# Weight sums moved into the attention in 2 KB pieces, and a scheduler's table of durations changed, in a two-layer diffusion block on one core

## The chip, the core and the metric

One NeuronCore of one Trainium2 chip runs the whole program in one launch. The metric is the time of one execution in microseconds (us) on the device. Five queues of instructions run beside each other: PE (matrix products), DVE and POOL (elementwise work), ACT (activations, scaled copies) and SP, which here only issues DMAs. POOL issues DMAs too. All DMAs of both queues share 16 DMA engines.

## The reference, cut to what matters

Two layers over 1024 latent and 256 context tokens of width 1024. Each projects the modulated input, runs latent attention (4 heads) and differential attention (4 heads) and a chunk mixer side by side, projects back, normalizes, and ends with a gated feed-forward block of inner width 2816 with a depthwise convolution of width 3:

```python
def conv_ffn(h, p):
    u = dwconv3(h @ p["ffn_wup"], p["ffn_convw"], p["ffn_convb"])
    gate, val = jnp.split(u, 2, axis=-1)
    return (jax.nn.silu(gate) * val) @ p["ffn_wdown"]

def layer(x, xc, mod, modc, rows, cols, p, layer_idx, need_ctx):
    sh1, sc1, g1, sh2, sc2, g2 = jnp.split(mod, 6, axis=-1)
    ...
    y, yc = mixer(x * (1.0 + sc1) + sh1, xc * (1.0 + csc1) + csh1, rows, cols, p, layer_idx, need_ctx)
    x = layer_norm(DN_ALPHA * x + g1 * y, p["ln1_g"], p["ln1_b"])
    x = layer_norm(DN_ALPHA * x + g2 * conv_ffn(x * (1.0 + sc2) + sh2, p), p["ln2_g"], p["ln2_b"])
```

`mod` comes from one more product, of the conditioning vector with `ada_w`; most of its columns are computed in pieces between the blocks of the attention.

## The kernel before, in words

Every fp32 product is three products of a high and a low half (`mm3`): each operand is copied into a high half (a rounding copy, on ACT or DVE; helpers `copy` L460 and `move` L466) and a low half (full minus high, helper `low` L457, on DVE or POOL). PE's own calls are all in the helper `mm` (L447).

The two feed-forward products use seven block products in place of eight (a scheme of Strassen's kind). That needs sums and differences of blocks of the weights. They are not computed on an engine: POOL issues DMAs that copy a block from DRAM to DRAM (L592, a copy) and then add another block into it (L593, an accumulating DMA; it waits for its copy, or for another sum). The arrays are `ws` for the first product and `db` for the second; each layer has 32 DMAs for `ws` and 16 for `db`, each of 1408 KB (`SUMROWS` rows of the flattened array). Later SP loads `ws` and `db` like any weight.

When the sums are issued: `sums` makes a list of calls (`self.due`) and `begin_sums(1)` takes the next. Before the change the `ws` of layer 0 begin in the input projection (every fourth tile, outside `z`) and go on as fillers in its attention; the `db` of layer 0 and the `ws` of layer 1 are issued in the first feed-forward product of layer 0 (`ffn`), the rest of the latter in the input projection and the attention of layer 1; the `db` of layer 1 in the first feed-forward product of layer 1. The key `MODKEY` puts them behind about 120 later pieces of work.

What sets the order: nothing is written out by hand. `Sched.run` is a list scheduler that runs while the program is built. Each piece of work is a task with a list of engines that may take it and a duration on each, from small formulas (`act_t`, `dve_t`, `pool_t`, `either` for DVE or POOL, `psum_copy` for ACT or DVE). It keeps a clock for each engine, and a free engine takes the ready task with the lowest key. The order so found is fixed in the program: on the chip each engine runs its list in order and waits on semaphores. So a formula changes no work, only which engine does a task, and when it stands in the list. A POOL DMA is a task of 1.0 us that is done 40 us later.

Other lines that the text names: L1018 and L1024 rotate the keys into a buffer whose store to `zd` must land before the buffer is used again; L1237 and L1238 join the two score maps of the differential attention on POOL, and L1262 is PE's transposition of the result; L1640 and L1650 combine products of the first feed-forward product out of PSUM; L1671 and L1673 are its convolution (ACT, then DVE); L1490 is elementwise work of the feed-forward block (DVE or POOL), among it the combinations that `store_pair` writes to `da`.

## Time and profile before

| | |
|---|---|
| time, median of 3 runs (us) | 3523.48 (3515.53 to 3527.67) |
| the profiled execution: its time, its span (us) | 3522.21, 3520.4 |
| granted TensorE clock, mean | 0.957 |
| PE busy (us, share) | 3210.6 (91%) |
| DVE | 2586.0 (73%) |
| ACT | 1652.2 (47%) |
| POOL | 1045.3 (30%) |
| DMA: SP's queue, POOL's queue (share of 16 engines) | 34.1%, 15.9% |

The page cuts the span into 40 slices. The stages, read from the first and the last instruction of lines that belong to one stage alone: input projection of layer 0 up to 312 us, attention to 870, output projection to 1020, first feed-forward product to 1670, second to about 1925, then layer 1: input projection to 2183, attention to 2670, output projection to 2795, first feed-forward product to 3265, second to the end. PE is the busiest engine in every stage; what it does not do in a stage stands in its idle time and in the share of the clock that it was granted.

### The profile page before, as it was taken

The page shows a single profiled execution, that of the slowest core. Times are in us where ns is not written, and L with a number is a line of the kernel's source. Part 1 is how long each engine was busy: PE and PEld are TensorE (multiplying, and loading weights), DVE is VectorE, ACT ScalarE, POOL GpSimd, SP SyncE. Part 2 cuts the span into 40 slices and gives each one's busy share as a digit, 9 for nine tenths or more (in the row PEclk, how much of TensorE's full clock was granted, in tenths as well). Part 3 has the DMA queues.
Part 4 walks back from the last instruction along what each step waited for, and adds up shares of the span by engine and source line. Part 5 has one row for each costly group of instructions (what it writes and reads, how often), then busy time and mean ns, then how long its engine had stood idle before and what let it go on. Part 6 is the DMA issues. An engine that isn't in the chain of part 4 may idle for free. (4 is left out here: it accounts for less than half of the span.)

```text
span 3520.4 us, 53639 instructions
## 1 busy us (share of the span) xinstructions
PE 3210.6 (91%) x18953; PEld 2801.2 (80%) x18953; DVE 2586.0 (73%) x6262; ACT 1652.2 (47%) x2931; POOL 1045.3 (30%) x678
## 2 busy tenths in 40 slices
PE   7799999998988889989998899999998889999997
PEld 5798888787977777777886799888888867788775
DVE  7456988988777566657569737889898776666687
ACT  5024666565344344434435404566663445454543
POOL 3101555553122111213034301454434232212143
PEclk9899999999999999999999999999998999999998
DMA  8823444443345666664765743132313556653672
GB/s 324 206 65 100 116 120 131 120 106 104 111 145 168 191 176 181 191 173 147 225 217 188 213 130 78 49 77 82 89 53 121 163 157 200 201 163 132 222 263 102
DMA packets 274839, 528.07 MB, mean 150 GB/s; under 512 B 67465, under 2 KB 119177, under 8 KB 264585
## 3 DMA queue, kind: packets, MB, share of 16 engines
q1 hardware_dynamic: 263048, 386.22, 34.1%
q0 software_dynamic: 11520, 138.42, 15.9%
q8 instruction: 149, 2.44, 0.3%
q14 instruction: 122, 0.99, 0.1%
HBM read 444.25 MB, written 218.69 MB: 188 GB/s over the span
## 5 line engine op out<-in xcount | busy, mean ns | idle before, releaser
L447 PE MATMUL t<-region 128*128 128x256 f32 (+4 forms) x15631 | 2876.0, 342 | 233.4 <-DVE region L457 69.7
L447 PEld LDWEIGHTS t<-region 128*128 128x128 f32 x15631 | 2458.0, 194 | 584.9 <-DVE region L457 82.6
L457 DVE TENSOR_TENSOR region<-region 128x512 fp32r<-128x512 f32 (+6 forms) x867 | 765.2, 907 | 267.8 <-ACT region L460 225.0
L460 ACT ACTIVATE region<-t 128x512 fp32r<-128x512 f32 (+4 forms) x935 | 452.6, 511 | 717.1 <-PE t L447 326.0
L460 ACT ACTIVATE region<-region 128x512 fp32r<-128x512 f32 (+4 forms) x944 | 591.2, 662 | 384.8 <-PE t L447 131.9
L457 POOL TENSOR_TENSOR region<-region 128x512 fp32r<-128x512 f32 (+5 forms) x289 | 403.9, 1408 | 1123.2 <-ACT region L460 804.6
L1490 POOL TENSOR_TENSOR region<-region 128x512 f32<-128x512 f32 (+2 forms) x107 | 212.0, 1984 | 911.3 <-ACT region L460 355.2
L1673 DVE SCALAR_TENSOR_TENSOR region<-region,conv 128x1023 f32<-128x1023 f32 x176 | 233.4, 1327 | 165.6 <-ACT region L1671 165.3
L1198 ACT ACTIVATE region<-region,q 128x1280 f32<-128x1280 f32 (+1 forms) x216 | 273.5, 1267 | 165.2 <-DVE q L1197 148.7
L1193 DVE TENSOR_SCALAR_CACHE_REDUCE region<-t 128x512 f32<-128x512 f32 (+1 forms) x600 | 333.6, 586 | 9.4 <-PE t L447 8.0
L457 DVE TENSOR_TENSOR region<-t,region 128x512 fp32r<-128x512 f32 (+1 forms) x529 | 297.8, 598 | 46.4 <-ACT region L460 41.6
L1262 PE MATMUL t<-ident,region 128*128 128x128 f32 x1312 | 186.1, 285 | 19.9 <-DVE region L1193 5.0
L1238 POOL TENSOR_TENSOR region<-region 128x1280 f32<-128x1280 f32 (+1 forms) x69 | 188.4, 2731 | 5.8
L1262 PEld LDWEIGHTS t<-ident,region 128*128 128x128 f32 x1312 | 154.9, 147 | 27.6 <-DVE region L1193 8.2
L1671 ACT ACTIVATE region<-region,conv 128x1024 f32<-128x1024 f32 x88 | 109.2, 1241 | 128.2 <-DVE region L1654 56.7
L1237 POOL TENSOR_SCALAR region<-region,q 128x1280 f32<-128x1280 f32 (+1 forms) x69 | 87.4, 1267 | 205.6 <-DVE q L1232 128.2
L447 PE MATMUL t<-region,s 128*4 128x256 f32 x768 | 118.2, 291 | 17.2 <-ACT region L460 10.8
L1490 DVE TENSOR_TENSOR region<-region 128x512 f32<-128x512 f32 (+2 forms) x150 | 113.3, 760 | 18.4 <-POOL region L1490 15.3
L1018 DVE TENSOR_TENSOR region<-t,region 128x256 f32<-128x256 f32 x32 | 13.6, 424 | 126.5 <-PE t L447 69.6
L447 PEld LDWEIGHTS t<-region,s 128*4 128x4 f32 x768 | 64.8, 87 | 46.4 <-ACT region L460 11.3
L548 POOL TENSOR_TENSOR region<-region 128x1024 f32<-128x1024 f32 x26 | 72.8, 2815 | 93.3 <-DMA region<-n 65.6
L1688 ACT ACTIVATE region<-region 128x1024 f32<-128x1024 f32 x66 | 53.4, 839 | 63.9 <-DVE region L1673 63.9
(137 smaller groups left out, 1849.5 us busy)
## 6 DMA issues: line engine op xcount, KB each, us to landing
ws<-in_wup POOLq DMA_DIRECT2D x48, 1408.0 KB, 9.8
region<-ws SPq DMA_DIRECT2D x176, 256.0 KB, 3.7
region<-in_ada_w SPq DMA_DIRECT2D x160, 256.0 KB, 3.5
region<-in_wup SPq DMA_DIRECT2D x154, 256.0 KB, 3.0
da<-region SPq DMA_DIRECT2D x154, 256.0 KB, 3.7
region<-da SPq DMA_DIRECT2D x154, 256.0 KB, 4.0
db<-in_w_down POOLq DMA_DIRECT2D x24, 1408.0 KB, 8.5
ws<-ws POOLq DMA_DIRECT2D x16, 1408.0 KB, 14.3
```

Of the source, the lines that this page charges most:

```text
L447: self.nc.tensor.matmul(ps, a, b, start=start, stop=stop, skip_group_check=again)
L457: eng.tensor_tensor(out=out, in0=full, in1=hi.bitcast(F32), op=ALU.subtract)
L460: self.nc.scalar.activation(out, in_, AF.Copy, **kw)
L548: self.task(engs or pool_t(D), lambda e, row=row, op=op: self.vec[e].tensor_tensor(out=x[:, :D], in0=x[:, :D], in1=row.t, op=op), [x, row] ...
L1193: self.task(dve_t(b - a), lambda e: nc.vector.tensor_scalar(p[:, a:b], ps[:, :b - a], -scale, None, op0=ALU.mult, op1=ALU.min, accum_out=n ...
L1198: self.task(act_t(nk, 0.19), lambda e: nc.scalar.activation(p[:, :nk], p[:, :nk], AF.Exp, bias=m.t, scale=-1.0, accum_out=s.t), [p, m], [p ...
L1237: nc.gpsimd.tensor_scalar(p2[:, :nk], p2[:, :nk], cc.t, 0.0, op0=ALU.mult, op1=ALU.add)
L1238: nc.gpsimd.tensor_tensor(out=p1[:, :nk], in0=p1[:, :nk], in1=p2[:, :nk], op=ALU.add)
L1262: nc.tensor.transpose(ps[:, u, j * P:(j + 1) * P], B[key][j][:, (kt + u) * P:(kt + u + 1) * P], self.ident)
L1490: self.task(either(n), lambda e: self.vec[e].tensor_tensor(out=o(), in0=a(), in1=b(), op=op), r, w, **kw)
L1671: self.task(act_t(n, 0.15), lambda e: nc.scalar.activation(t.t, u(0, n), AF.Identity, scale=c[:, 1:2], bias=c[:, 3:4]), r + ["conv"], [t])
L1673: self.task(dve_t(n - 1, extra=0.06), lambda e, d=d: nc.vector.scalar_tensor_tensor(t[:, 1 - d:n - d], u(d, n - 1 + d), c[:, 2 * d:2 * d + ...
```

## The change

Three things. (1) The sums of a layer, `ws` and `db`, are all issued among the fillers of that layer's attention; the calls in the input projection and in the feed-forward block are gone. (2) Their arrays are seen as rows of 512 numbers (2 KB), 704 to a DMA, for copies and accumulations alike. The bytes and the number of DMAs stay. Before, a copy stood as 32 rows of 11264 numbers and an accumulation as 176 rows of 2048. The memory that holds the descriptors of POOL's DMAs grows from 1024 to 2048 bytes. (3) The formulas of durations: POOL from 2.1 to 2.5 ns per element, DVE in `either` and for the weights of the first product from 1.042 to 1.35, ACT's high halves from 0.833 to 1.03, the convolution longer.

```diff
-SUMROWS = 176
+SUMROWS = 704
...
 def pool_t(n):
-    return {"pool": 2.1e-3 * n + 0.15}
+    return {"pool": 2.5e-3 * n + 0.15}
...
+def act_r(n):
+    return {"act": 1.03e-3 * n + 0.09}
+def dve2_t(n):
+    return dve_t(n, 1.35e-3)
 def either(n):
-    return {**dve_t(n), **pool_t(n)}
+    return {**dve2_t(n), **pool_t(n)}
...
     def flat(self, x, c):
-        return x.rearrange("n p c -> (n p c)").rearrange("(r c) -> r c", c=2048)[c * SUMROWS:(c + 1) * SUMROWS]
+        return x.rearrange("n p c -> (n p) c")[c * SUMROWS:(c + 1) * SUMROWS]
...
-            out.append(lambda: self.s.add({"pool": 1.0}, lambda e: self.nc.gpsimd.dma_start(out=put(), in_=self.flat(a(), c)), (), **kw))
-            out.append(lambda: self.s.add({"pool": 1.0}, lambda e: self.nc.gpsimd.dma_start(out=put(), in_=self.flat(b(), c), accum_op=ALU.add, max_dma_last_dim=8192), [*r, key], **kw))
+            out.append(lambda: self.s.add({"pool": 1.0}, lambda e: self.nc.gpsimd.dma_start(out=put(), in_=self.flat(a(), c), max_dma_last_dim=2048), (), **kw))
+            out.append(lambda: self.s.add({"pool": 1.0}, lambda e: self.nc.gpsimd.dma_start(out=put(), in_=self.flat(b(), c), accum_op=ALU.add, max_dma_last_dim=2048), [*r, key], **kw))
...
-            if name != "z" and n % 4 == 1:
-                self.begin_sums(1)
...
-            if f >= 2 and (x[1] == "22" or l == 0 and f % 2 and x[1] == "S2"):
-                self.begin_sums(1)
...
+            self.due = self.sums(l, "ws") + self.sums(l, "db")
...
-    nc = _bacc.Bacc("TRN2", target_bir_lowering=False, num_devices=1, dynamic_dma_scratch_size=1024)
+    nc = _bacc.Bacc("TRN2", target_bir_lowering=False, num_devices=1, dynamic_dma_scratch_size=2048)
```

How it moves instructions, at three places on POOL. In the rows below `region` is any working buffer and `q` a column of statistics (a number behind a name tells buffers apart), `ws` and `db` are the arrays of sums; lines of the changed program are 6 to 8 higher (L457 is L465, L592 and L593 are L600 and L601, L1237 and L1238 are L1243 and L1244, L1490 is L1496).

POOL at the start of the program (input stage), before:

```order
L457 TENSOR_TENSOR region<-region 128x1024 x3
L592 DMA ws<-in_wup 32x11264 x5
L457 TENSOR_TENSOR region<-region 128x768
L457 TENSOR_TENSOR region<-region 128x256 x4
L457 TENSOR_TENSOR region<-region 128x1280
L457 TENSOR_TENSOR region<-region 128x768
L457 TENSOR_TENSOR region<-region 128x1280
L457 TENSOR_TENSOR region<-region 128x768
L592 DMA ws<-in_wup 32x11264
```

POOL at the same place, of the change:

```order
L465 TENSOR_TENSOR region<-region 128x1024 x6
L465 TENSOR_TENSOR region<-region 128x256
L465 TENSOR_TENSOR region<-region 128x768
L465 TENSOR_TENSOR region<-region 128x256 x4
L465 TENSOR_TENSOR region<-region 128x1280
L465 TENSOR_TENSOR region<-region 128x768
L465 TENSOR_TENSOR region<-region 128x1280
L465 TENSOR_TENSOR region<-region 128x768
L465 TENSOR_TENSOR region<-region 128x1280
```

The five copies at the start, and the sixth a little later, have left; the low halves follow each other. The first sum of the change stands behind the input projection.

POOL in the middle of the attention of layer 0, before:

```order
L1237 TENSOR_SCALAR region_8793<-region_8793,q_8899 128x1280
L1238 TENSOR_TENSOR region_8765<-region_8765,region_8793 128x1280
L1237 TENSOR_SCALAR region_8843<-region_8843,q_8944 128x1280
L1238 TENSOR_TENSOR region_8817<-region_8817,region_8843 128x1280
L457 TENSOR_TENSOR region_2796<-region_6044,region_8554 128x512
L593 DMA ws_91<-ws_91 176x2048
L457 TENSOR_TENSOR region_8554<-region_7603,region_2796 128x512
L457 TENSOR_TENSOR region_5388<-region_6044,region_353 128x512
L1237 TENSOR_SCALAR region_8992<-region_8992,q_9152 128x1280
L1238 TENSOR_TENSOR region_6044<-region_6044,region_8992 128x1280
L1237 TENSOR_SCALAR region_9055<-region_9055,q_9230 128x1280
L1238 TENSOR_TENSOR region_7812<-region_7812,region_9055 128x1280
```

POOL in the attention of layer 0, of the change, where the sums of `ws` run out and the first of `db` begins:

```order
L1243 TENSOR_SCALAR region_6307<-region_6307,q_6400 128x1280
L1244 TENSOR_TENSOR region_6274<-region_6274,region_6307 128x1280
L601 DMA ws_91<-ws_91 704x512
L465 TENSOR_TENSOR region_5291<-region_4597,region_5550 128x512
L601 DMA ws_91<-in_wup 704x512 x2
L600 DMA ws_91<-in_wup 704x512
L465 TENSOR_TENSOR region_2787<-region_6109,region_5496 128x512
L465 TENSOR_TENSOR region_2837<-region_6129,region_2786 128x512
L465 TENSOR_TENSOR region_3008<-region_6129,region_5856 128x512
L600 DMA db_93<-in_w_down 704x512
L465 TENSOR_TENSOR region_3199<-region_6109,region_3198 128x512
L465 TENSOR_TENSOR region_6665<-region_4597,region_6665 128x2x2x32 x2
```

Both pieces begin at the joins of a block of the attention. Before, one DMA stands between the joins of this block and those of the next; of the change five stand behind the joins, three of them with no work between. Counted over the whole order, 48 stand in either attention, where the attentions had 14 and 5 by the trace.

POOL in the first feed-forward product of layer 0, before:

```order
L1490 TENSOR_TENSOR region_10068<-region_10068,region_11779 128x1024
L1490 TENSOR_TENSOR region_11580<-region_10068 128x512
L1490 TENSOR_TENSOR region_12303<-region_12303,region_11620 128x1024
L1490 TENSOR_TENSOR region_11779<-region_12303,region_11779 128x128
L1490 TENSOR_TENSOR region_12035<-region_11779,region_12035 128x128
L1490 TENSOR_TENSOR region_11580<-region_12035,region_10068 128x512
L592 DMA db_93<-in_w_down 32x11264
L1490 TENSOR_TENSOR region_11580<-region_11580,region_11620 128x1024
L593 DMA db_93<-db_93 176x2048
L592 DMA db_93<-in_w_down 32x11264
L1490 TENSOR_TENSOR region_12783<-region_12783,region_11620 128x1024
```

POOL at the same place, of the change:

```order
L1496 TENSOR_TENSOR region_11248<-region_11248 128x1024
L1496 TENSOR_TENSOR region_11640<-region_12059,region_11640 128x128
L1496 TENSOR_TENSOR region_10412<-region_11673,region_11248 128x512
L1496 TENSOR_TENSOR region_11248<-region_10412,region_11673 128x512
L1496 TENSOR_TENSOR region_11640<-region_11248 128x512
L1496 TENSOR_TENSOR region_10412<-region_10412,region_11248 128x1024
L1496 TENSOR_TENSOR region_12826<-region_10412 128x512
L1496 TENSOR_TENSOR region_12889<-region_12889 128x1024
```

The DMAs have left, and more of the combinations of 512 columns stand on POOL. Over the whole program 28 of these go from DVE to POOL, and 27 high halves out of PSUM of 512 columns (L466) go from DVE to ACT.

## Rows read from the trace of the kernel before

**Rows 1.** The whole core by stages, one row each: attention of layer 0, the first feed-forward product of layer 0, attention of layer 1, the first feed-forward product of layer 1. A row gives the stretch in us, its length, then for each engine the busy time and the number of instructions, and last the granted TensorE clock, the busy share of the 16 DMA engines and GB/s.

```profile
312.00:870.00 558.00, 514.01 (x3594) 457.54 (x3594) 493.97 (x1466) 346.14 (x685) 269.74 (x185) 0.96 0.41 113
1020.00:1670.00 650.00, 579.38 (x2894) 484.72 (x2893) 422.26 (x520) 273.19 (x445) 144.16 (x102) 0.96 0.61 175
2183.00:2670.00 487.00, 448.60 (x3124) 400.93 (x3125) 434.68 (x1242) 300.57 (x560) 219.95 (x131) 0.96 0.29 81
2795.00:3265.00 470.00, 439.77 (x1907) 355.87 (x1907) 319.22 (x362) 232.97 (x356) 110.51 (x60) 0.97 0.57 175
```

**Rows 2.** The DMA view of the stretch from 45 to 180 us: the two queues (q0 is the one that POOL issues on, q1 that of SP) with packets, MB and share of the 16 engines' time, and one group of issues with its median us from issue to landing.

```profile
q0 software_dynamic: 1728, 21.63, 59.6%
q1 hardware_dynamic: 6095, 10.19, 22.9%
zd<-region SPq DMA_DIRECT2D x7, 128.0 KB, 33.6
```

**Rows 3.** The DMA view of the attention of layer 0 (312 to 870 us): SP's queue.

```profile
q1 hardware_dynamic: 42761, 42.07, 25.6%
```

**Rows 4.** The timeline of POOL from 108 to 176 us, some of its rows in order: start, us, engine, line, operation, count, and in brackets the idle time ahead of it and what ended that.

```profile
110.56 1.90 POOL L593 DMA_DIRECT2D ws<-in_wup  x2
125.39 0.88 POOL L593 DMA_DIRECT2D ws<-in_wup  x1 [6.67 <-issue]
125.98 3.25 POOL L457 TENSOR_TENSOR region<-region 128x1280 fp32r<-128x1280 f32 x1
141.18 0.88 POOL L593 DMA_DIRECT2D ws<-ws  x1 [6.66 <-issue]
```

**Rows 5.** The timeline of DVE from 118 to 175 us, one row.

```profile
171.41 0.43 DVE L1018 TENSOR_TENSOR region<-t,region 128x256 f32<-128x256 f32 x1 [39.83 <-DMA zd<-region]
```

**Rows 6.** The timeline of PE, nine rows that follow an idle stretch (in brackets: its length and what ended it).

```profile
83.99 1.94 PE L447 MATMUL t<-region 128*128 128x64 f32 x8 [6.72 <-issue]
90.34 1.94 PE L447 MATMUL t<-region 128*128 128x64 f32 x8 [4.41 <-issue]
172.50 3.74 PE L447 MATMUL t<-region 128*128 128x256 f32 x16 [19.43 <-DVE region L1024]
977.42 7.75 PE L447 MATMUL t<-region 128*128 128x256 f32 x45 [7.80 <-ACT region L460]
1030.95 4.23 PE L447 MATMUL t<-region 128*128 128x512 f32 x17 [3.21 <-DVE region L457]
1544.85 3.36 PE L447 MATMUL t<-region 128*128 128x512 f32 x7 [7.72 <-DVE region L1650]
2011.92 4.37 PE L447 MATMUL t<-region 128*128 128x64 f32 x14 [10.66 <-DVE q L499]
2809.72 2.50 PE L447 MATMUL t<-region 128*128 128x256 f32 x10 [4.34 <-ACT region L460]
2897.95 2.50 PE L447 MATMUL t<-region 128*128 128x512 f32 x5 [4.79 <-DVE region L1650]
```

**Rows 7.** Four more stretches in the view by windows: 18 us in the input stage, 8 us in the first feed-forward product of layer 0, the end of that stage, and the greater part of the same stage in layer 1.

```profile
80.00:98.00 18.00, 9.59 (x34) 8.48 (x35) 18.00 (x64) 2.08 (x3) 8.95 (x5) 0.53 0.43 147
1186.00:1194.00 8.00, 5.14 (x15) 4.13 (x16) 5.12 (x7) 2.89 (x5) 0.00 (x0) 0.57 0.69 237
1584.00:1670.00 86.00, 81.08 (x405) 67.38 (x405) 63.94 (x73) 42.87 (x70) 26.95 (x16) 1.00 0.47 145
2904.00:3260.00 356.00, 348.91 (x1506) 280.67 (x1505) 236.47 (x274) 178.14 (x266) 73.83 (x36) 1.00 0.57 175
```

**Rows 8.** The DMA view of the first feed-forward product of layer 0 (1020 to 1670 us) and of layer 1 (2795 to 3265 us): the stores of the gated product, median us to landing last.

```profile
da<-region SPq DMA_DIRECT2D x74, 256.0 KB, 9.9
da<-region SPq DMA_DIRECT2D x72, 256.0 KB, 2.3
```

**Rows 9.** The view of waits in the first feed-forward product of layer 0: who waited for whom, us in total, times, longest.

```profile
PE t L447 <- DVE region L1650: 36.3, 8, 7.7
ACT region L1671 <- DMA da<-region: 48.7, 8, 11.6
```

**Rows 10.** The timeline of POOL from 1168 to 1190 us: two issues.

```profile
1171.74 0.55 POOL L592 DMA_DIRECT2D db<-in_w_down  x1
1172.28 0.95 POOL L593 DMA_DIRECT2D db<-in_w_down  x1
```

**Rows 11.** The source view of the two issuing lines in the attention of layer 0: duration of the issuing instruction in ns (min/median/max), first and last start, and for each line the us to landing (min/median/max).

```profile
L592 POOL DMA_DIRECT2D ws<-in_wup x7: 553/581/587, 352.2 to 689.7; - x7
DMA to landing us min/median/max: 6.0/7.4/7.7
L593 POOL DMA_DIRECT2D ws<-ws x4: 891/907/946, 462.9 to 764.7; - x4
DMA to landing us min/median/max: 9.9/10.1/10.7
```

**Rows 12.** The view of waits in the attention of layer 0 and in that of layer 1: PE waiting for POOL's half of the joins, the whole list of PE's waits for POOL over 0.5 us.

```profile
PE t L1262 <- POOL region L1238: 0.8, 1, 0.8
PE t L1262 <- POOL region L1238: 3.5, 1, 3.5
```

**Rows 13.** Groups by line and form over the whole span, and the source view of line 466 in the attention of layer 0: the two operations that change their engine.

```profile
L1490 POOL TENSOR_TENSOR region<-region 128x512 f32<-128x512 f32 x60 | 93.2, 1556 | 184.2 <-ACT region L1515 75.3 <-DVE region L457 26.5 <-DVE q L478 18.1
L466 DVE CAST region<-t x56: 666/679/692, 364.6 to 842.2; 128x512 fp32r<-128x512 f32 x56
```

More of the change, by code (lines that the diff above doesn't have):

```diff
@@ L362 @@
 HI_EMIT = dve_fast
-HI_W = act_t
+HI_W = act_r
 HI_PV = psum_copy
@@ L468, in split @@
     def split(self, n, hi, lo, full, r, wh, wl, engs=None, high=None, **kw):
-        self.task(high or act_t(n), lambda e: self.move(e, hi(), full()), r, [wh], **kw)
+        self.task(high or act_r(n), lambda e: self.move(e, hi(), full()), r, [wh], **kw)
         self.task(engs or dve_t(n), lambda e: self.low(self.vec[e], lo(), full(), hi()), list(r) + [wh], [wl], **kw)
@@ L591, in make @@
             kw = dict(w=[key], key=MODKEY, late=40.0)
-            out.append(lambda: self.s.add({"pool": 1.0}, lambda e: self.nc.gpsimd.dma_start(out=put(), in_=self.flat(a(), c)), (), **kw))
-            out.append(lambda: self.s.add({"pool": 1.0}, lambda e: self.nc.gpsimd.dma_start(out=put(), in_=self.flat(b(), c), accum_op=ALU.add, max_dma_last_dim=8192), [*r, key], **kw))
-        for c in range((NF if which == "ws" else NP) * P * 512 // (SUMROWS * 2048)):
+            out.append(lambda: self.s.add({"pool": 1.0}, lambda e: self.nc.gpsimd.dma_start(out=put(), in_=self.flat(a(), c), max_dma_last_dim=2048), (), **kw))
+            out.append(lambda: self.s.add({"pool": 1.0}, lambda e: self.nc.gpsimd.dma_start(out=put(), in_=self.flat(b(), c), accum_op=ALU.add, max_dma_last_dim=2048), [*r, key], **kw))
+        for c in range((NF if which == "ws" else NP) * P * 512 // (SUMROWS * 512)):
             at = lambda n: (which, l, n, c)
@@ L616, in sum_chunks @@
         a, b = f * P * 512, (f + 1) * P * 512 - 1
-        m = SUMROWS * 2048
+        m = SUMROWS * 512
         return [(name, l, n, c) for c in range(a // m, b // m + 1)]
@@ L899, in in_chunk @@
             tiles = (8, 9, 0, 1) if l == 0 else (6, 7, 8, 9, 2, 3, 4, 5)
-        for n, t in enumerate(tiles):
-            if name != "z" and n % 4 == 1:
-                self.begin_sums(1)
+        for t in tiles:
             r = self.in_tile(l, name, t, wk, wb, tabs)
@@ L1587, in up_operand @@
         raw, self.up_raw[m] = self.up_raw[m], None
[L1588 removed]
+        self.blocks[f][n] = self.parts(HALF, lambda: raw.t, [raw], engs=dve2_t(HALF))
     def up_mm(self, ps, x, y, first, acq=(), h=None):
@@ L1797, in ffn @@
         last = order[-1][1]
-        assert not self.due
-        self.due = self.sums(l, "db") + (self.sums(1, "ws") if l == 0 else [])
         done = 0
@@ L1907, in program @@
         self.first_hT()
-        self.due = self.sums(0, "ws")
         for l in range(DEPTH):
```

5 lines of the change are left out of this document (2 added, 3 removed).

## The prediction, made before the run

> **What bounds the kernel now.** I read the windows by stage first. In both attentions and in both first feed-forward products PE is busy for over nine tenths of the stretch, or just under it [rows 1], so the kernel can only gain what PE loses: its idle time, and the time in which its clock is granted at 0.5. In the first product of layer 0 that is 650 - 579.4 = 70.6 us of idle time. Then the DMA view, because POOL's queue is what the change rearranges. From 45 to 180 us POOL's queue holds 59.6% of the 16 engines' time and SP's 22.9%, and a store to `zd` needs 33.6 us to land [rows 2]. What that does stands in two timelines: DVE stands still for 39.83 us because a `zd` store has not landed and its buffer is not free [rows 5], and PE behind it for 19.43 us at 172.5 us [rows 6]. Last, the timeline of PE gap by gap. The large gaps stand behind sums: POOL issues two at 1171.74 and 1172.28 us [rows 10], and 10 to 17 us later the clock is at 0.57 and PE works 5.14 of 8 us [rows 7]. In the same stage the stores to `da` land after 9.9 us, against 2.3 us in layer 1 [rows 8]; ACT waits 48.7 us for them, and PE 36.3 us, in eight gaps, for the DVE line L1650 that stands behind ACT's convolution [rows 9].
>
> Why a sum starves SP's loads and stores: its pieces are long. Before, a copy has 32 pieces of 45 KB, an accumulation 176 of 8 KB, while a 256 KB load has pieces of 2 KB. [...]
>
> **The change part by part.**
>
> *Sums leave the start, the projections and the feed-forward products.* What can come back is the gaps behind sums, and half of PE's busy time at a clock near 0.5 right after them. Input stage and projection of layer 0: 6.72 + 4.41 + 19.43 = 30.6 us of gaps; in the 18 us at 0.53, 9.59 us busy, of which 4.5 would go at full clock [rows 6, 7], and some 2 us more behind the third gap, as an estimate from the same row. At most 37; I take 30, since SP's own loads fill the engines at first. Output projection of layer 0: 7.80 us and about 2 at half clock; I take 8. First product of layer 0: eight gaps from the one that ends at 1030.95 (3.21) to the one at 1544.85 (7.72) [rows 6]. As a check from the other side, the end of that stage, after the last sum, has PE busy 81.08 of 86 us at a clock of 1.00 [rows 7]. At that rate the stage would idle 5.7% of 650 = 37 us in place of 70.6, and the clock would rise from 0.96 to 1.00, worth up to 4% of 579 = 23: 57 in all. I take 48. Input projection of layer 1: 10.66 and about 2; I take 11. First product of layer 1: gaps from 4.34 to 4.79 [rows 6], four of them, of some 15 us together by those two bounds, and about 6 at half clock; I take 18. From 2904 us on that stage works at 348.91 of 356 us with sums still in it [rows 7], so nothing more is there, and it shows that a sum does not always cost PE. Sum taken: 115 us. Bounds: about 60 (half of the gaps were due to something else) and 140.
>
> *48 sums in either attention, where 14 and 5 stood.* The issuing instruction costs POOL 0.58 us for a copy and 0.91 for an accumulation [rows 11]; for four to 22 times as many pieces it is between that and, by the step of 0.33 us over 144 more pieces (here 528 to 672 more), about 2.1. That alone is 48 x 0.75 = 36 to 100 us per attention on an engine that is busy for 270 of 558 and 220 of 487 us [rows 1]; the cover is there.
>
> The price that I look at most is room. After two accumulations at 110.56 us, POOL does not issue the third until 125.39 us, sits idle for 6.67 us of that with "issue" as the only reason, and holds a ready subtraction (L457 at 125.98) behind it; the same again at 141.18 [rows 4]. Two accumulations of 11 pieces per engine fit, the third waits until the first has landed. The change has 44 pieces per engine in twice the room: one accumulation fits, two do not, and a copy beside it is near the edge. So sums go nearly one at a time, and POOL, which issues in order, stands still when the next comes early. A copy lands after 7.4 us, an accumulation after 10.1 [rows 11]. Going through POOL's order of the change with these, and with the mean durations of its work between two sums (on average 5.4 us in layer 0, that is 270 less its 14 issues, over 48; 4.5 in layer 1), 25 and 27 of the 48 have to wait, 8 us each: about 200 us in layer 0 and 215 in layer 1. POOL is then taken for 260 + 36 + 200 = 496 of 558 us and 216 + 36 + 215 = 467 of 487. It does not become longer than the attention, but it is nearly full.
>
> Who waits behind it: low halves of weights and queries, and the joins, for PE. At present PE waits for the joins 0.8 and 3.5 us in the two attentions [rows 12], so they are ready in good time and a delay of some us is mostly hidden. For what PE loses I take 1 us for each of the 52 waits, 55 with the clock after it, from between nothing (all hidden) and 150 (SP's 25.6% [rows 3] stretches each landing by a quarter and an issue costs 2.1 us: POOL needs about 600 and 580 us, 45 and 90 beyond the present stages, and some for clock). It is nearer to nothing, because a wait of 8 us falls on an engine that has been idle half the time.
>
> *Pieces of 2 KB.* The bytes stay, so I price a copy and an accumulation as they are. Were the price one per piece and not per byte, an accumulation would take four times 10.1 us; against that, SP moves its 256 KB in 2 KB pieces and lands in 2.3 us at 8 pieces per engine [rows 8], under 0.3 us for each, at most 44 x 0.3 = 13 us for 44. That upper end lies in the 150.
>
> *Durations.* 27 high halves of 0.679 us go from DVE to ACT, 18 us, and 28 combinations to POOL at 1.556 us, 44 us [rows 13], in stages where POOL is busy for 144 of 650 and 111 of 470 us [rows 1]. DVE, at 494 of 558 us in the attention of layer 0, gets air. What a new order makes of that I can't price; I take nothing, from -15 to +20.
>
> [...]
>
> Sum: 3522.2 (the time of the profiled execution; its span is 3520.4, and the median of the runs is 1.3 above it) - 115 + 55 = 3462 us.
>
> **The rivals.** (a) *POOL's waits are hidden*: the attention loses 0 to 20 us, the rest comes back: about 3400 to 3425 us. For it: the joins wait for nobody. Against it: five sums in a row behind one block. (b) *POOL becomes the bound in the attention*: landings of 12 to 13 us instead of 10, so that POOL's list is longer than the attention's other work; the place is the pair of accumulations without work between. It decides from a loss of 126 us on, that is when each of the 52 waits costs PE 2.2 us; at 150 to 200 us it gives 3557 to 3607. [...] (c) *Half and half*: the gaps in the feed-forward products have other reasons (in layer 1 the same sums cost nothing from 2904 us on), 60 us come back and 60 go: about 3522. (d) *The sums don't matter outside*: only the input stage gains, 30 us, against 55: about 3547.
>
> **How the numbers follow.** Two executions differ by some 0.3%, or 10.6 us; less than that is no change here. Chances: the forecast (3430 to 3500 us) 0.46, (a) 0.20, (c) 0.12, (b) 0.17, (d) 0.05. Faster is the forecast and (a), 0.66; same is (c), 0.12; slower is (b) and (d), 0.22. The likeliest case's own range is 3430 to 3500. For 8 in 10 the range takes in most of (a) and the near half of (b): 3390 to 3565.
>
> **What the profile of the changed kernel would show.** Right: no DVE wait on a `zd` store in the input stage; stores to `da` landing after about 2 to 3 us in both layers; PE's waits for L1650's line gone, and the clock at 1.00 through most of the first products; these two stages 45 and 20 us shorter; POOL idle before its sums with "issue" for about 200 us in either attention, and both attentions 20 to 35 us longer. Wrong: stage times outside the attention as before, gaps of PE in the first product without a sum near them; or attentions over 60 us longer, with PE waiting for POOL's joins or low halves in tens of us; or landings of 2 KB accumulations above 13 us.

## The result, and the profile after

The changed kernel takes 3570.9 us (median; 3567.5 to 3576.2) against 3524.4 us before: a ratio of 1.0137 (95% interval 1.0114 to 1.0161). It is slower by 1.4%, 6 us above the upper end of the range.

| | after |
|---|---|
| the profiled execution: its time, its span (us) | 3567.46, 3565.7 |
| granted TensorE clock, mean | 0.945 |
| PE, DVE, ACT, POOL busy | 90%, 72%, 47%, 31% |
| DMA: SP's queue, POOL's queue | 33.6%, 16.9% |

All the work is still there, and PE's busy time is 12 us longer than before; the loss is waiting, and the lower clock around it. The table gives the length of each stage in us, in the traces of the kernels of this study (e1 to e14 are the experiments below). The boundaries are read from the first or last instruction of one line per stage (numbers of the kernel before): the last of the norm of the latent keys (L955) ends the projection, the last of L1193 the attention, the first of L1640 the output projection, its last the first product, the last of L1768 the second; in layer 1 that stage goes on to the end of the span. By these boundaries the two first products before are 44 and 49 us shorter than in [rows 1], and the attentions 10 us shorter and 1 us longer.

```
                       layer 0                      layer 1
                       in   att   out  up  down     in   att  out  up  down   span
before                 308  548   185  606  266     265  488  167  421  268   3520
after                  280  655   183  525  270     260  536  185  400  271   3566
e1  old durations      285  652   182  531  268     257  555  180  411  273   3594
e2  new durations      296  542   190  542  276     266  486  160  413  270   3442
e3  room 4096          284  597   183  525  270     260  533  184  401  272   3511
e4  8 KB pieces        283  625   183  525  271     260  578  182  404  271   3581
e5  16 rows            284  550   185  525  269     260  468  181  401  274   3397
e6  before + 2 KB      293  554   185  541  267     271  492  160  412  267   3441
e7  all but the move,  286  542   191  538  272     257  487  157  402  272   3404
    room 4096
e9  half rows          284  559   183  525  271     260  479  179  404  270   3415
e10 all but the move   294  540   187  523  275     278  488  157  402  273   3416
e8  new durations,     292  544   187  542  273     256  487  164  408  273   3426
    8 KB
e11 move, old pieces   282  631   183  525  271     260  579  181  404  271   3587
e12 rest in second     287  542   191  540  285     260  481  158  410  273   3425
    product
e13 ada early          281  643   196  525  261     263  562  159  401  272   3563
e14 ada early, tiny    283  587   197  525  261     263  507  157  401  272   3453
```

From before to after, everything outside the two attentions is 112 us shorter (28 of it in the input stage, 81 in the first product of layer 0, 21 in that of layer 1; the output projection of layer 1 is 18 longer). The attentions are 107 and 48 us longer, 155 together. That makes the 45 us between the spans, but for rounding.

By the trace not all 48 sums of a layer stand in its attention: the first five are issued in the last 63 and 54 us of the input projection, 43 after it.

The view by windows of the changed kernel: attention of layer 0, first product of layer 0, attention of layer 1, its output projection, its first product. It answers to [rows 1].

```profile
280.00:935.00 655.00, 530.47 (x3545) 465.93 (x3544) 481.84 (x1410) 352.00 (x697) 280.18 (x197) 0.88 0.63 160
1118.00:1643.00 525.00, 518.36 (x2710) 443.79 (x2709) 382.43 (x467) 252.04 (x404) 122.89 (x70) 0.99 0.41 127
2174.00:2710.00 536.00, 467.37 (x3130) 412.15 (x3129) 423.54 (x1237) 307.22 (x571) 251.23 (x167) 0.92 0.71 174
2710.00:2895.00 185.00, 152.55 (x1128) 148.32 (x1126) 124.41 (x396) 64.00 (x106) 42.27 (x28) 0.88 0.31 100
2895.00:3295.00 400.00, 390.55 (x1695) 318.55 (x1694) 309.89 (x316) 209.03 (x313) 102.97 (x49) 0.99 0.42 136
```

The first products are nearly full: PE is busy for 518 of 525 and 391 of 400 us at a clock of 0.99. In the attentions PE stands idle for 125 and 69 us, at clocks of 0.88 and 0.92 where 0.96 stood, and the DMA share went from 0.41 to 0.63 and from 0.29 to 0.71.

The first product gained where it was said to. The stores to `da` in layer 0, which took 9.9 us to land [rows 8]:

```profile
da<-region SPq DMA_DIRECT2D x72, 256.0 KB, 3.3
```

PE's and ACT's waits of [rows 9] for L1650's line and for these stores are gone from the list of that stage.

The waits in the attention of layer 0 after the change: PE for low halves of DVE and of POOL, ACT for loads of `ada_w`, and POOL before a sum with "issue" as the only reason (us in total, times, longest).

```profile
PE t L455 <- DVE region L465: 42.6, 21, 13.2
PE t L455 <- POOL region L465: 43.2, 7, 11.7
ACT region L468 <- DMA region<-in_ada_w: 50.6, 14, 18.6
POOL ws L600 <- issue: 48.4, 6, 11.8
POOL ws L601 <- issue: 31.8, 5, 11.0
POOL db L601 <- issue: 21.1, 2, 12.9
POOL db L600 <- issue: 20.1, 3, 10.2
```

POOL stands still before 16 sums, 121 us in all, and PE now waits for low halves up to 13.2 us at a time. One such chain, from the timelines of POOL, ACT, DVE and PE:

```profile
580.76 1.18 POOL L601 DMA_DIRECT2D ws<-ws  x1
594.25 1.25 POOL L601 DMA_DIRECT2D ws<-in_wup  x1 [11.01 <-issue]
605.59 1.12 POOL L601 DMA_DIRECT2D ws<-in_wup  x1 [10.08 <-issue]
616.10 0.71 POOL L600 DMA_DIRECT2D ws<-in_wup  x1 [9.39 <-issue]
616.81 1.28 POOL L465 TENSOR_TENSOR region<-region 128x512 fp32r<-128x512 f32 x1
...
620.55 0.38 ACT L468 ACTIVATE region<-t 128x256 fp32r<-128x256 f32 x1 [18.87 <-POOL region L465]
...
620.97 0.76 DVE L465 TENSOR_TENSOR region<-t,region 128x256 fp32r<-128x256 f32 x2 [19.77 <-ACT region L468]
...
621.87 0.82 PE L455 MATMUL t<-region 128*128 128x256 f32 x2 [13.17 <-DVE region L465]
```

POOL issues an accumulation at 580.76 us, and the next three must each wait some 10 us: these accumulations land 13.2, 11.0 and 10.2 us after their issue, and the DMA behind each is issued 13.5, 11.3 and 10.5 us after it. The low half at 616.81 stands behind them (rows left out are marked by three dots). ACT waits 18.87 us for it, DVE's low half waits for ACT for 19.77, and PE for DVE for 13.17.

In the output projection of layer 1, PE waits once for a reload of a normalized tile (the view of waits), and SP's timeline shows why:

```profile
PE t L1423 <- DMA region<-n: 13.4, 1, 13.4
```

```profile
2809.71 1.55 SPq L452 DMA_DIRECT2D region<-in_wup  x2
2811.36 1.45 SPq L452 DMA_DIRECT2D region<-n  x2
```

SP issues two such reloads at 2811.36, behind loads of weights. In layer 1 the output projection is 18 us longer than before. The gap, 13.2 to 13.8 us, is in the changed kernel and in e1, e3, e4, e5, e9 and e11. It is in no trace with the sums at their old places, and not in e13 and e14, which have the attention's list in another order; there the stage is 157 to 167 us long. Since e5, almost without the sums' bytes, has it too, it comes with the order of the list and not from their traffic.

### The profile page after: what moved, and what is told of

Its sections match the earlier page's. It is cut to its first block, busy times and chain, and to the rows that moved or that the text cites. A ratio compares the mean times of both kernels' runs of the same rounds, so it can differ in the third digit from the quotient of the medians.

```text
span 3565.7 us, 53607 instructions
## 1 busy us (share of the span) xinstructions
PE 3222.5 (90%) x18953; PEld 2817.2 (79%) x18953; DVE 2578.5 (72%) x6215; ACT 1671.6 (47%) x2958; POOL 1100.9 (31%) x698
## 3 DMA queue, kind: packets, MB, share of 16 engines
q1 hardware_dynamic: 263048, 386.22, 33.6%
q0 software_dynamic: 52224, 138.42, 16.9%
## 5 line engine op out<-in xcount | busy, mean ns | idle before, releaser
L465 DVE TENSOR_TENSOR region<-region 128x512 fp32r<-128x512 f32 (+6 forms) x882 | 789.8, 919 | 204.5 <-ACT region L468 130.8
L468 ACT ACTIVATE region<-t 128x256 fp32r<-128x256 f32 (+4 forms) x962 | 465.4, 515 | 743.3 <-PE t L455 395.5
L465 POOL TENSOR_TENSOR region<-region 128x512 fp32r<-128x512 f32 (+5 forms) x274 | 392.7, 1456 | 866.5 <-ACT region L468 534.4
L1496 POOL TENSOR_TENSOR region<-region 128x512 f32<-128x512 f32 (+1 forms) x142 | 264.9, 1871 | 806.2 <-DVE region L1679 543.5
L465 DVE TENSOR_TENSOR region<-t,region 128x512 fp32r<-128x512 f32 (+1 forms) x529 | 298.4, 596 | 76.5 <-ACT region L468 75.5
L1268 PE MATMUL t<-ident,region 128*128 128x128 f32 x1312 | 183.1, 284 | 10.1 <-DVE q L487 5.2
L1244 POOL TENSOR_TENSOR region<-region 128x1280 f32<-128x1280 f32 (+1 forms) x69 | 189.1, 2741 | 5.8
L1243 POOL TENSOR_SCALAR region<-region,q 128x1280 f32<-128x1280 f32 (+1 forms) x69 | 91.8, 1330 | 157.4 <-DVE q L1238 90.8
L1496 DVE TENSOR_TENSOR region<-region 128x512 f32<-128x512 f32 (+3 forms) x115 | 93.1, 817 | 1.0 <-POOL region L1496 0.4
L1656 DVE SCALAR_TENSOR_TENSOR region<-t,region 128x512 f32<-128x512 f32 x44 | 30.3, 688 | 61.4 <-PE t L455 61.4
## 6 DMA issues: line engine op xcount, KB each, us to landing
ws<-in_wup POOLq DMA_DIRECT2D x48, 1408.0 KB, 10.1
db<-in_w_down POOLq DMA_DIRECT2D x24, 1408.0 KB, 10.1
ws<-ws POOLq DMA_DIRECT2D x16, 1408.0 KB, 11.9
```

Source lines behind the costliest of these rows:

```text
L465: eng.tensor_tensor(out=out, in0=full, in1=hi.bitcast(F32), op=ALU.subtract)
L468: self.nc.scalar.activation(out, in_, AF.Copy, **kw)
L1243: nc.gpsimd.tensor_scalar(p2[:, :nk], p2[:, :nk], cc.t, 0.0, op0=ALU.mult, op1=ALU.add)
L1244: nc.gpsimd.tensor_tensor(out=p1[:, :nk], in0=p1[:, :nk], in1=p2[:, :nk], op=ALU.add)
L1268: nc.tensor.transpose(ps[:, u, j * P:(j + 1) * P], B[key][j][:, (kt + u) * P:(kt + u + 1) * P], self.ident)
L1496: self.task(either(n), lambda e: self.vec[e].tensor_tensor(out=o(), in0=a(), in1=b(), op=op), r, w, **kw)
```

## The experiments

Theory R: POOL stands still for descriptor room, and PE pays for it. Rivals: O, the new durations make a worse order in the attention; T, the sums' bytes slow SP's transfers in the attention, whoever waits for room. Ratios are to the kernel before on the same chip.

**The durations, undone and alone.** e1 takes the changed kernel with the old formulas; e2 is the kernel before with the new formulas:

```diff
-    return {"pool": 2.1e-3 * n + 0.15}
+    return {"pool": 2.5e-3 * n + 0.15}
...
-    return {**dve_t(n), **pool_t(n)}
+    return {**dve2_t(n), **pool_t(n)}
```

> The changed kernel with the old formulas of durations, sums and pieces as changed. Theory R (POOL stands still for room in its descriptor memory, and low halves and loads come late behind it): the order is another, but the sums are as many and as close, so the attentions stay within 30 us of the changed kernel's 667 and 515 us, and the time is 3540 to 3600 us. Rival O (the new table of durations makes a worse order in the attention): the attentions fall back to about 590 and 510 us, the time to 3440 to 3490 us. Rival T (the sums' traffic in the attention slows SP's loads, whoever issues it): as R.

> The kernel before with the new formulas of durations alone; sums stand where they stood, in old pieces, with the old room. R and T: within 20 us of the time before (3504 to 3544 us). O: slower by 50 us or more (over 3575 us), with the loss in the attentions.

e1: 3583.9 us, 1.0169 (1.0140 to 1.0198), as R and T had it: the attentions, 652 and 555 us, stay long without the new durations. e2: 3439.4 us, 0.9763 (0.9740 to 0.9786). O falls: the new durations cost nothing in the attentions (542 and 486 us against 548 and 488) and win 85 us alone, which no theory expected. Of that, 64 us come in the first product of layer 0, although its sums are still in it. In e2 the stores to `da` land there after 3.8 us, beside sums in their old pieces (DMA view of that stage):

```profile
da<-region SPq DMA_DIRECT2D x72, 256.0 KB, 3.8
```

**Room.** e3 gives the changed kernel twice the room, e4 longer pieces, of which at least four sums fit at once (an estimate from [rows 4], where two accumulations fit in half that room):

```diff
-dynamic_dma_scratch_size=2048)
+dynamic_dma_scratch_size=4096)
```

```diff
-        return x.rearrange("n p c -> (n p) c")[c * SUMROWS:(c + 1) * SUMROWS]
+        return x.rearrange("n p c -> (n p c)").rearrange("(r c) -> r c", c=2048)[c * SUMROWS:(c + 1) * SUMROWS]
...
-accum_op=ALU.add, max_dma_last_dim=2048)
+accum_op=ALU.add, max_dma_last_dim=8192)
```

> The changed kernel with 4096 bytes for descriptors in place of 2048; two accumulations of 44 pieces per engine and a copy then fit, as two accumulations fitted before the change. The order is the same. R: POOL's idle time before its sums with only issue as a reason falls from some 120 us in the attention of layer 0 to under 40, and most of the attentions' loss comes back: 3430 to 3490 us. O and T: within 20 us of the changed kernel (3550 to 3590 us).

> The changed kernel with copies and accumulations in pieces of 8 KB (11 per engine) in place of 2 KB, room 2048: four or five sums fit at once. R: no stall for room, the attentions come back as in the run with room 4096 or further: 3420 to 3490 us; it costs something if the longer pieces starve SP's loads. T: the same bytes at the same places, the attentions as slow as in the changed kernel or slower, 3550 to 3620 us. O: 3550 to 3590 us.

e3: 3515.0 us, 0.9975 (0.9961 to 0.9990). e4: 3577.6 us, 1.0155 (1.0130 to 1.0180). R's range is missed both times; T's holds for e4 and not for e3. Room gives back 58 us in the attention of layer 0 and 3 in that of layer 1, and the time stays above the range that R gave. In e3 the waits for room are nearly gone (view of waits, attention of layer 0, then of layer 1), but ACT waits as long or longer for `ada_w` (39.9 us in layer 1 in the changed kernel):

```profile
POOL ws L601 <- issue: 12.8, 2, 10.2
ACT region L468 <- DMA region<-in_ada_w: 50.5, 18, 8.4
POOL db L600 <- issue: 3.4, 1, 3.4
ACT region L468 <- DMA region<-in_ada_w: 66.6, 20, 10.8
```

In e4 POOL hardly waits for room any more (0.2 us in both attentions together), and still they are slower than in e3 by 28 and 45 us; ACT waits 68.3 and 100.8 us there for `ada_w`. Its median landing of `ada_w` is no later than in e3 (4.6 us, below), but the loads of `wk` are (9.3 us in e3). DMA view from 290 to 880 us in e4:

```profile
region<-in_ada_w SPq DMA_DIRECT2D x88, 256.0 KB, 4.3
region<-in_wk SPq DMA_DIRECT2D x3, 128.0 KB, 19.7
```

**The bytes.** e5 keeps the changed kernel's order on every engine, but each sum moves 16 of its 704 rows; e9 moves 352, with room 4096. So most or half of each sum is left out, and the two feed-forward products read, in place of sums, blocks of the weights of the same size:

```diff
-dma_start(out=put(), in_=self.flat(b(), c), accum_op=ALU.add,
+dma_start(out=put()[:16], in_=self.flat(b(), c)[:16], accum_op=ALU.add,
...
-                src, r = self.ws[l][j, f], self.sum_chunks("ws", l, j, f)
+                src, r = self.i["wup"][l, j // 2, j % 2, f], self.sum_chunks("ws", l, j, f)
```

> The changed kernel in the same order on every engine, room 2048, but each of the 96 sums moves 16 of its 704 rows (one piece per engine), and the loads of sums read a block of the weights of the same size instead; so the sums are left out but for a trace of them. R + T (room for descriptors, and then the sums' traffic beside the loads of the attention): neither is left, the attentions fall from 655 and 536 us to 535 to 555 and 480 to 495, the time to 3400 to 3440 us. O2 (the order is what costs: 48 sums between POOL's low halves, or the pieces of the list that moved): the attentions stay above 580 and 515 us, the time above 3480.

> The changed kernel with room 4096 and its order, each sum moving 352 of 704 rows (so half of the sums are left out, and the loads of sums read a block of the weights of the same size instead). It stands between the run with room 4096 (attentions 597 and 533 us, time 3515) and the one with 16 rows (550 and 468 us, 3398). T in proportion (each piece in flight delays the attention's loads by its time): about half way, 570 to 580 and 495 to 505 us, 3450 to 3470 us. T with slack (a load has some us to spare, only the long jams reach PE): near the lower end, 3400 to 3430 us. I (POOL's time for the issues, 0.7 and 1.1 us each, and not the bytes): the issue gets shorter by the pieces, half way too, but without waits of ACT for the loads of ada_w.

e5: 3397.9 us, 0.9638 (0.9624 to 0.9653). That is even more than R + T forecast: 2 us below its range of times, with the attention of layer 0 in its range (550 us) and that of layer 1 12 us below (468). So 48 short sums in either list cost next to nothing as instructions (the attentions before are 548 and 488 us long). e9: 3418.4 us, 0.9692 (0.9654 to 0.9730), T with slack: the first half of the bytes costs the attentions 9 and 11 us, the second 38 and 54. So of the 173 us that the changed kernel's attentions are longer than those of e5, 61 go with more room (58 + 3), and the other 112 (47 + 65) only with fewer bytes. In layer 1 room is worth little: POOL waits 129 us for room there in the changed kernel and 3.4 in e3, at nearly the same stage time. That the bytes then bind fits this.

One rival is that POOL's time for issuing is what costs, since fewer rows also mean shorter issues: POOL is busy for 269.9 and 242.5 us in the attentions of e5, and for 278.6 and 252.2 in those of e3 (windows). e4 decides against it: its POOL is busy for less than that of e3 as well, at most 271.3 and 243.1 us, with the same bytes, and its attentions are longer. The order is no rival either: PE, DVE, ACT, POOL and SP run the same list of instructions in the changed kernel, e3, e4 and e11, and in e5 and e9 but for the blocks that the loads of sums read.

How the bytes act stands in the DMA view from 290 to 880 us, about the attention of layer 0 (queues with packets, MB and share; then KB and median us to landing); in e9 and e5 it takes in 37 and 46 us of the output projection. e3, whole sums:

```profile
q0 software_dynamic: 23200, 60.56, 44.2%
region<-in_ada_w SPq DMA_DIRECT2D x88, 256.0 KB, 4.6
region<-in_cst SPq DMA_DIRECT2D x17, 128.0 KB, 7.1
yt<-region SPq DMA_DIRECT2D x19, 64.0 KB, 7.3
region<-zd SPq DMA_DIRECT2D x17, 64.0 KB, 5.5
```

e9, half:

```profile
q0 software_dynamic: 11936, 30.28, 22.8%
region<-in_ada_w SPq DMA_DIRECT2D x88, 256.0 KB, 3.7
region<-in_cst SPq DMA_DIRECT2D x17, 128.0 KB, 4.0
yt<-region SPq DMA_DIRECT2D x20, 64.0 KB, 2.1
```

e5, 16 rows:

```profile
q0 software_dynamic: 1344, 1.38, 1.5%
region<-in_ada_w SPq DMA_DIRECT2D x88, 256.0 KB, 3.2
region<-in_cst SPq DMA_DIRECT2D x17, 128.0 KB, 2.5
yt<-region SPq DMA_DIRECT2D x20, 64.0 KB, 1.7
region<-zd SPq DMA_DIRECT2D x17, 64.0 KB, 2.4
```

With POOL's queue at 44% of the 16 engines' time, tables from `cst` land after 7.1 us instead of 2.5, stores to `yt` after 7.3 instead of 1.7. With half the bytes most of that is gone. Whether the short transfers wait at the DMA engines or for the memory was not separated.

**Pieces, and the move.** e6 is the kernel before with 2 KB pieces and room 2048 alone; e10 has the new durations too, so it is the change without its move; e7 is e10 with room 4096; e8 has the new durations with copies of 8 KB; e11 is the changed kernel with old pieces and old room; e12 is e7 with the sums of layer 1 that are left after the first product issued in the second:

```diff
+                if l == 0 and p in (0, NP // 2):
+                    self.begin_sums(1)
```

> The kernel before with pieces of 2 KB and room 2048 alone: sums where they stood, old durations. A (long pieces hold up SP's loads and stores, wherever the sums stand): the first feed-forward product of layer 0 falls from 606 to 530 to 560 us, the input stage by 10 to 20, the stores to da land after 2 to 4 us; the attention of layer 0 loses up to 20 us for room (14 sums); 3430 to 3480 us. T (it is the bytes that compete, not the length of a piece): the stage stays at 590 us or more, the time at 3500 to 3550 us.

> The kernel before with the new durations, pieces of 2 KB and room 4096; against the run with room 4096 it differs only in where the sums stand. A: the input stage falls from 296 to about 285 us, the first product of layer 0 from 542 to about 528, the attentions stay at 542 and 486: 3405 to 3430 us. T: what the pieces give is not more than what the bytes take, 3430 to 3460 us.

> The kernel before with the new durations, copies in pieces of 8 KB in place of 45 KB, accumulations as they were, room 2048. A: between the run with the new durations alone (3439) and that with 2 KB pieces: 3415 to 3440 us. T: 3430 to 3450 us.

> The change without its move: new durations, pieces of 2 KB, room 2048, sums where they stood before. R (room costs only where POOL's sums stand close and PE needs POOL's next output): the sums outside the attention stand behind little that PE needs, so within 15 us of the run with room 4096 (3407): 3400 to 3425 us. Rival: room 2048 stalls POOL in the first product too, 3430 to 3470 us. Either way the move costs the difference to 3571.

> The changed kernel with the old pieces (copies of 45 KB, accumulations of 8 KB) and the old room 1024: the move and the new durations alone. T (the bytes of the sums beside the attention's loads, long pieces worse): attentions as with 8 KB pieces or longer, 625 to 680 and 575 to 620 us, 3570 to 3640 us. Rival (the loss comes from the 2 KB pieces and their descriptors): the attentions at 545 to 570 and 485 to 500 us, 3400 to 3450 us.

> New durations, pieces of 2 KB, room 4096, sums as before the change, but the 14 to 34 sums of layer 1 that are left after the first product of layer 0 are issued in its second product, not in the projection and the attention of layer 1. If the sums in the attention of layer 1 cost it the 19 us between 487 and 468: 3385 to 3405 us. If that difference is the order's, or the second product's loads suffer as much: 3405 to 3430 us.

```
                                            sums at their old places         sums in the attention
old durations, old pieces, room 1024        3524 (before)                    not run
old durations, 2 KB, room 2048              3444, 0.9766 (e6)                3584, 1.0169 (e1)
new durations, old pieces, room 1024        3439, 0.9763 (e2)                3588, 1.0174 (e11)
new durations, 8 KB, room 2048              3429, 0.9729 (e8)                3578, 1.0155 (e4)
new durations, 2 KB, room 2048              3424, 0.9713 (e10)               3571, 1.0137 (after)
new durations, 2 KB, room 4096              3407, 0.9672 (e7)                3515, 0.9975 (e3)
```

In every row with both sides run the right one is slower, by 108 to 149 us. A's ranges of time hold for e6, e7 and e8, R's for e10, T's for e11; T, which in e6 had the first product at 590 us or more, is wrong there (541). Pieces with their room alone win 81 us and durations alone 85, together 105 at room 2048 (beside 3529 for the kernel before on that chip), since either wins most of the same gaps in the first product of layer 0: 65 and 64 us there, and 83 together. In e6 the stores there land after 6.6 us, later than A expected:

```profile
da<-region SPq DMA_DIRECT2D x72, 256.0 KB, 6.6
```

e12 takes 3418.4 us, 0.9693 (0.9661 to 0.9725), no better than e7: the attention of layer 1 gains 6 us (481), and the second product of layer 0 loses 13 (285). e7 is the best version with whole sums: 3406.9 us, 3.3% faster than before (0.9672, 0.9651 to 0.9693).

**By which transfers.** ACT's waits for `ada_w`, 50.5 and 66.6 us in e3 and 0.6 and 3.1 in e5, suggested that the bytes reach PE through these loads alone. In e13 (room 4096) and its twin e14 (16 rows per sum) the pieces of that product are called ahead of the attention, so that their loads end early in it:

```diff
-                fill += [lambda: self.begin_sums(1)] * (...) + [a]
+                fill += [lambda: self.begin_sums(1)] * (...)
+            for a in ada:
+                a()
             self.attention(l, fill)
```

> The changed kernel with room 4096, but the pieces of the product with ada_w are called ahead of the attention, so that their loads bunch in its first part; the sums stay spread over the whole attention. To be compared with its twin with 16 rows per sum. L (the sums cost PE by way of the loads of ada_w, for which ACT waits in the middle of the attention's own copies): the difference to the twin in the attentions falls from 47 and 65 us (the runs with room 4096 and 16 rows) to under 25 and 30. X (any load, or POOL's issuing itself): it stays at 40 to 65 us in both.

> The twin: the same order on every engine, 16 of 704 rows per sum (the sums are left out but for a trace of them, and the loads of sums read a block of the weights of the same size instead). Both theories: attentions within 25 us of 550 and 468 us; the earlier pieces may cost something at the start.

e13: 3564.2 us, 1.0101 (1.0081 to 1.0121). e14: 3452.4 us, 0.9790 (0.9775 to 0.9805). The attentions are 643 and 587, 562 and 507 us long: the bytes cost 56 and 55 us, near the 47 and 65 of e3 against e5. (e14's own expectation failed: its attentions are 37 and 39 us longer than those of e5, not within 25, so calling the pieces early has a price of its own.) The windows of the stretch behind the last of these loads in the attention of layer 0, with the same work, in e13 and in e14:

```profile
471.00:924.00 453.00, 395.72 (x2633) 353.07 (x2631) 367.79 (x1141) 254.36 (x488) 187.00 (x134) 0.93 0.69 166
```

```profile
454.00:870.00 416.00, 382.19 (x2645) 343.68 (x2643) 367.44 (x1141) 253.96 (x489) 176.63 (x134) 0.97 0.17 45
```

It is 37 us longer, at a clock of 0.93 in place of 0.97. So the loads of `ada_w`, which have ended, are not the only way. The landings in it, e13 and then e14:

```profile
region<-in_cst SPq DMA_DIRECT2D x17, 128.0 KB, 7.2
yt<-region SPq DMA_DIRECT2D x18, 64.0 KB, 7.0
region<-zd SPq DMA_DIRECT2D x17, 64.0 KB, 8.7
```

```profile
region<-in_cst SPq DMA_DIRECT2D x17, 128.0 KB, 2.7
yt<-region SPq DMA_DIRECT2D x18, 64.0 KB, 1.6
region<-zd SPq DMA_DIRECT2D x17, 64.0 KB, 2.5
```

Some of DVE's waits for transfers there in e13; the list of e14 has none:

```profile
DVE region L1168 <- DMA region<-in_cst: 9.5, 3, 4.0
DVE region L1300 <- DMA yt<-region: 7.3, 2, 4.8
DVE region L1178 <- DMA region<-zd: 5.5, 3, 3.2
```

But e13 and e14 differ in one thing more. In e13 POOL waits for room again, 32 us in this stretch and 64 us in the attention of layer 1, and in e14 it does not; two groups of these waits in the stretch:

```profile
POOL ws L600 <- issue: 17.5, 3, 8.5
POOL db L600 <- issue: 9.8, 1, 9.8
```

So the 37 us are those of late landings and of room together. What share each of these waits has in PE's loss was not separated.

## Why the prediction was wrong, step by step

**The gaps that come back** (115 us): 112 measured, outside the attentions. Input stage 28 (30 forecast), first product of layer 0 81 (48), of layer 1 21 (18), output and input projections 2 and 5 (8 and 11); the output projection of layer 1 lost 18, which no step had. The places were right, and the total came out right partly by luck: the first product of layer 0 gave 33 us more than forecast, and the output projection of layer 1 and the second products, for which no step had a loss, took 25 back. (The 15 us for four gaps in layer 1 are their sum in the trace; by the two bounds named, 4.34 and 4.79, they would be 17 to 19.) What was wrong is to book the gain as the move's: at the old places, new durations or shorter pieces alone bring 64 and 65 of these 81 us (e2, e6). Against e10, with all else equal, the move brings the input stage 14 us, the projection of layer 1 18, and the first product of layer 0 nothing; it costs the attentions 115 and 48 us and the output projection of layer 1 28.

**Durations** ("I take nothing, from -15 to +20"): 85 us won alone, far outside these bounds. I had counted the work that changes engines and not what the order does to stores and loads that wait for each other: the landings of `da` are 3.8 us in e2 against 9.9 [rows 8], and PE's waits for L1650's line fall from 36.3 us [rows 9] to 6.4. By which step the new order does this was not shown.

**Room** (52 waits at 1 us, 55 us): the rows show 16 and 15 waits, 121 and 129 us, where I had 25 and 27, and some 200 and 215. An accumulation lands after 11.9 us (median), where I had taken 10.1 [rows 11] as it was, and the issuing instruction takes 0.71 and 1.14 us, within its bounds. The source view of L601 in the attention of layer 0:

```profile
DMA to landing us min/median/max: 10.2/11.9/15.0
```

One reason for fewer waits: I gave a copy 44 pieces per engine like an accumulation. In e5, with 16 rows, 42 sums have 1344 packets, 32 each, so 16 come on top of the rows. The 23200 packets of e3 above are then those of 22 accumulations at 704 + 16 and 20 copies at 352 + 16, so by these counts a copy goes in pieces of 4 KB, 22 per engine. Two copies fit in 2048 bytes (in the changed kernel POOL issues one at 616.10 us, which lands after 7.6 us, and the next at 620.46 us), and a copy beside an accumulation does not (616.10 in the chain).

What more room gives back is 61 us. So fewer waits cost some 2 us each in place of 1, and that the product came out near the forecast is luck. The sentence "a delay of some us is mostly hidden" did not hold for three sums in a row, as in the chain shown. (In rival (b), 126 us over 52 waits are 2.4 us each, not 2.2, unless the clock has a share.)

**The term that was missing** is the sums' bytes beside the attention's own transfers: 112 us, which the sum had at nothing. Read from the stage table, the account is 3522, less 112 outside, less 18 (the attentions of e5 are together 18 us shorter than those before), plus 61 for room and 112 for bytes: 3565 us, which is the measured time but for rounding, as all four come from the same table. I had let SP's traffic stretch the sums' landings, and never the reverse, though [rows 2] and [rows 8] showed just that elsewhere. The step that failed is to take the bytes as free once the pieces are short: beside whole sums in short pieces SP's transfers land 1.4 to 4.3 times as late as beside 16 rows of each (e3 against e5: `ada_w` 4.6 and 3.2 us, `yt` 7.3 and 1.7). How an engine divides its time between the two queues no run shows.

**The rivals.** The time lies in the range of (b), 3557 to 3607, and its landings of 12 to 13 us are nearly there. But its mechanism carries only a part: with POOL's waits alone the time would be about 3522 - 112 - 18 + 61 = 3453. (c) and (d), by which the sums don't matter outside, fall by e6, where shorter pieces alone give 65 us in the first product of layer 0; but (c) has a point in e2, where 64 us come back with the sums untouched.

**The signs.** Of the signs of being right, DVE's wait of 39.83 us for a `zd` store in the input stage [rows 5] is gone, and the first products became shorter. Of those of being wrong, one came: the attentions are 107 and 48 us longer, and in that of layer 0 PE waits 43.2 and 42.6 us for low halves. Here too the bytes are most of it, and room the rest: 47 and 58 us in that attention.

## What to carry to other kernels

Before moving DMAs into a stage, price them against that stage's own small loads and stores, not only against the engine that issues them: here half of the bytes cost 20 us and all of them 112. A stage that looks idle in its DMA share (0.41, 0.29) may need that idleness to have its loads and stores land soon (1.7 to 3.2 us in e5's rows). Where a change has several parts, cost each alone: here two of three parts each won over 2%, and the third lost over 3%.

## What the runs showed of the hardware

- In the changed kernel POOL stood still before 16 sums in the attention of layer 0, 121 us in all, and what stood behind them in its list waited too. In the chain above each DMA was issued 0.3 us after the accumulation before it had landed. Twice the room (4096 bytes, e3), with the same list, cut these waits to 12.8 us.
- A full room was not always a loss. With the sums at their old places, room 2048 (e10) makes POOL wait 96 us in the input stage and 67 in the projection of layer 1, and these are 8 and 21 us longer than with 4096 (e7); but the first product of layer 0 is 15 us shorter. That sums held back leave the stage's loads alone there is a guess that was not tested.
- The price of the bytes was not in proportion: POOL's queue at 22.8% of the engines' time (e9) cost the attention of layer 0 9 us against e5, at 44.2% (e3) 47 us.
- Rows of 2 KB did not make the same pieces of both kinds: by the packet counts a copy went in 352 pieces of 4 KB and an accumulation in 704 of 2 KB. In 2048 bytes of room at most one accumulation or two copies were in flight at a time, over all 96 of the changed kernel. In 4096 (e3) two accumulations were issued at 561.68 and 563.65 us, and the third, behind 10.17 us of idle time, at 575.41.
